# A decoder trunk whose first projection sums the even feature blocks first, and whose last store goes out in two halves

## The chip, the cores and the metric

The kernel runs on one core of one Trainium2 chip. The metric is the time of one execution in device microseconds (us); the time before is the median of 3 runs. PE is the matrix engine, PEld its weight loads, DVE, ACT and POOL are the vector, scalar and general engines, and SP is the engine whose queue issues the kernel's DMAs.

## What is computed

A trunk of two layers over 1024 tokens of width 1024, batch 1. In layer 0 the normalised input is multiplied by one wide matrix, and its columns go to two token mixers; the change touches the first 384 of the columns that feed the attention (queries, keys and values of heads 0 and 1), and the very last addition of layer 1.

```python
def even_mixer(h, w_in, ...):
    z = h @ w_in                       # sum over 1024 features
    u, v, q, k, vb = jnp.split(z, ...)
    ...                                # gMLP of u, v; QK-norm attention of q, k, vb
    return jnp.concatenate([a_out, b_out], axis=-1) @ w_out

def reference(x, ...):
    for layer in range(2):
        h = rms_norm(x, norm_mix_g[layer])
        mix = even_mixer(h, ...) if layer % 2 == 0 else gla_mixer(h, ...)
        x = x + mix
        h = rms_norm(x, norm_ffn_g[layer])
        x = x + conv_ffn(h, ...)
    return x
```

All is float32. A product is made of three passes over parts: each operand is split into a rounded high part and the remainder as a low part, and high by high, high by low and low by high are added up (`PASSES`).

## The kernel before, in words

Tokens are cut into 8 tiles of 128, features into 8 blocks of 128. The program is one long list of instructions that a scheduler orders for each engine before it runs; engines then run their lists strictly in order and wait for one another by semaphores. So a change in one place may re-order the lists for a good way behind it.

**The start.** `x_T` holds each token tile with features on the partitions, even blocks (0, 2, 4, 6) first and odd blocks behind them. `features(n)` (L543 to L552) loads a tile and splits it into `hq[0]` (even blocks) and `hq[1]` (odd blocks), ACT making the high part (L101) and DVE the low part (L102). For the odd halves of tiles 0 and 1 POOL makes the high part. Tile 0 is loaded in two halves (`cut`), tile 1 in one piece. `token_rows(n)` (L536) loads the same tile with tokens on the partitions, and `statistics` squares and sums its rows on ACT (L533), which POOL makes into the scale `r0` of each token (L141, L142). `load_qkv(0, ...)` (L618) loads the first pair's weights in four DMAs of two feature blocks each and scales and splits each block (ACT L106, DVE L107), and calls `between` after each DMA is issued; that hook puts the tile loads between the weight loads. SP issues these DMAs in the order of its list, on one queue.

**The first pair's projection.** `projected(n)` (L773) sums tile n over feature blocks 0 to 7 in `mm_tok` (L193): 8 blocks by 3 passes, 24 matmuls of 128x384 for a tile. Behind it ACT makes the squares and the values (L780, L782), DVE the sums (L787), POOL the scales (L141, L142), DVE and POOL the scaled queries and keys (L789, L791), POOL and DVE their parts `qs` and `ks` (L101, L102). PE turns them (`tq` L809, `tk` L817), makes scores (`sc` L727), turns the exponentials (`pP` L747) and multiplies by the values (`po` L755). `early` lets three tiles be projected ahead of the first unit of attention; `rest` places the row statistics of later tiles. Projections of the next pair fill PE between the units of a pair.

**The end.** `ffn_down` (L384 to L426) makes the last matrix product in seven parts. The last one, part 4 of layer 1, leaves four sums of 128x512, one for each t. Each is added to the residual (DVE, L424) and stored by one DMA on SP (L1272).

## Time and profile before

| what | value |
|---|---|
| runs | 2151.78, 2152.53, 2155.79 us, median 2152.53 |
| the profiled execution, its own time | 2153.15 us |
| its span in the trace | 2151.4 us (1.75 us less) |
| PE busy | 2126.6 us, 99% |
| DVE busy, ACT busy, POOL busy | 1526.0 (71%), 1035.9 (48%), 482.4 us (22%) |
| mean DMA rate | 164 GB/s |
| PE share of the chain that ended last | 92% |

PE is busy all along, apart from the beginning, some short waits and the end. The busy time of the whole span therefore says little about this change: what counts is the first 60 us and the last 4 us. The timeline view gives each group of like instructions on an engine with its start, its length, its count, and in brackets the idle time before it and what ended that. The view of windows gives busy times of stretches, and in the column PEclk the clock that was granted to PE, as a share of full speed.

### The profile page before, as it was taken

To read this page: it belongs to the slowest core of one execution; us is meant where nothing else is said; L and a number is where in the kernel's file an instruction comes from. 1 tells how busy PE (TensorE), PEld (TensorE's weight loads), DVE (VectorE), ACT (ScalarE), POOL (GpSimd) and SP (SyncE) were. 2 spreads that over 40 slices of the span, in tenths; PEclk is the share of its full clock that TensorE was granted. 3 is DMA by queue.
4 is the path that set the end of the run, shared out by engine and by line. 5 is a ranking of instruction groups with operands and counts; after the bars stand their busy time and mean duration, and the time that the engine had idled before them with its cause. 6 is when DMAs were issued, how large, how long until landed. Compare 5 with 4: busy or idle time off the path is not lost.

```text
span 2151.4 us, 29696 instructions
## 1 busy us (share of the span) xinstructions
PE 2126.6 (99%) x10444; PEld 1804.0 (84%) x10444; DVE 1526.0 (71%) x2451; ACT 1035.9 (48%) x1998; POOL 482.4 (22%) x521
## 2 busy tenths in 40 slices
PE   8999999999999999999999999999999999999999
PEld 7999988888888888888898888888788888888887
DVE  7566655587888888655577777677778888885554
ACT  7555664365444444444454455535544444444443
POOL 5344310012424334000010011011234334220000
PEclk9999999999999999999999999999999999999999
DMA  7022313754444544765553233395554544457664
GB/s 273 24 77 68 104 40 120 256 195 156 155 161 158 176 143 157 255 237 192 206 183 113 74 105 102 133 307 206 177 167 161 168 153 154 162 181 280 215 216 166
DMA packets 159413, 353.70 MB, mean 164 GB/s; under 512 B 17392, under 2 KB 54256, under 8 KB 158880
## 3 DMA queue, kind: packets, MB, share of 16 engines
q1 hardware_dynamic: 159264, 351.81, 47.9%
q8 instruction: 82, 1.34, 0.3%
q14 instruction: 67, 0.55, 0.1%
HBM read 243.15 MB, written 108.59 MB: 163 GB/s over the span
## 4 chain that ended last, share of the span: by engine, by line
PE 92%; DVE 2%; ACT 2%; DMA 2%; issue 1%; SPq 0%; POOL 0%; DVEq 0%; ACTq 0%
PE puB L293 11%; PE pgB L293 11%; PE po L193 8%; PE pv L193 6%; PE pj L193 6%; PE puC L293 6%; PE pgC L293 6%; PE pdB L400 5%; PE pdC L400 5%; PE pdO L400 4%; PE puA L293 3%; PE pgA L293 3%; PE pdQ L400 2%; PE pdP L400 2%; PE pu L193 2%; PE pBq L1070 2%
## 5 line engine op out<-in xcount | busy, mean ns | idle before, releaser
L102 DVE TENSOR_TENSOR da<-ar,da 128x512 fp32r<-128x512 f32 x154 | 106.1, 689 | 154.2 <-ACT da L101 154.1
L101 ACT CAST da<-ar 128x512 fp32r<-128x512 f32 x154 | 95.9, 623 | 207.8 <-PE pdC L400 91.5
L193 PE MATMUL po<-wo,hq 128*128 128x512 f32 x768 | 184.0, 394 | 0.2 <-ACT hq L101 0.2
L193 PEld LDWEIGHTS po<-wo,hq 128*128 128x128 f32 x768 | 141.6, 188 | 29.6 <-DVE hq L102 1.1
L193 PE MATMUL pv<-wv,hq 128*128 128x512 f32 (+2 forms) x768 | 140.8, 340 | 1.6 <-DVE b L1102 1.6
L400 PE MATMUL pdB<-dw,da 128*128 128x512 f32 x528 | 135.5, 391 | 0.9 <-ACT u L308 0.7
L400 PE MATMUL pdC<-dw,da 128*128 128x512 f32 x528 | 135.1, 390 | 0.0
L193 PEld LDWEIGHTS pv<-wv,hq 128*128 128x128 f32 x768 | 118.7, 189 | 16.4 <-DVE b L1102 2.1
L400 PEld LDWEIGHTS pdB<-dw,da 128*128 128x128 f32 x528 | 98.7, 188 | 22.3 <-ACT u L308 1.1
L259 POOL TENSOR_TENSOR S1g<-rg 128x512 f32<-128x512 f32 x20 | 31.1, 1555 | 382.9 <-DMA wsd<-D 266.1
L400 PEld LDWEIGHTS pdC<-dw,da 128*128 128x128 f32 x528 | 99.0, 188 | 20.5
L102 DVE TENSOR_TENSOR dw<-wr,dw 128x512 fp32r<-128x512 f32 x154 | 105.6, 686 | 12.1 <-ACT dw L101 11.9
L193 PE MATMUL pj<-wq,hq 128*128 128x384 f32 x576 | 111.3, 341 | 0.0
L141 POOL TENSOR_SCALAR rn<-ssq 128x1 f32<-128x1 f32 x24 | 9.7, 403 | 446.1 <-ACT h L149 244.9
L101 ACT CAST dw<-wr 128x512 fp32r<-128x512 f32 x154 | 95.0, 617 | 15.7 <-DMA wr<-in_w_dn 9.3
L400 PE MATMUL pdO<-dw,da 128*128 128x512 f32 x396 | 102.2, 389 | 0.2 <-DVE dw L102 0.2
L193 PEld LDWEIGHTS pj<-wq,hq 128*128 128x128 f32 x576 | 99.9, 189 | 0.1
L400 PEld LDWEIGHTS pdO<-dw,da 128*128 128x128 f32 x396 | 74.2, 188 | 16.0 <-DVE dw L102 0.6
L322 DVE SCALAR_TENSOR_TENSOR t<-g,cw,t 128x1022 f32<-128x1022 f32 x44 | 76.6, 1742 | 0.1
L306 DVE TENSOR_TENSOR g<-g,s1g 128x512 f32<-128x512 f32 x22 | 16.2, 737 | 76.9 <-ACT s1g L305 76.9
L321 DVE SCALAR_TENSOR_TENSOR t<-g,cw,t 128x1023 f32<-128x1023 f32 x44 | 58.2, 1322 | 16.2 <-ACT t L320 16.1
L323 ACT ACTIVATE t<-t 128x1024 f32<-128x1024 f32 x44 | 46.7, 1061 | 29.7 <-DVE t L322 29.6
(1084 smaller groups left out, 5432.6 us busy)
## 6 DMA issues: line engine op xcount, KB each, us to landing
ar<-actd SPq DMA_DIRECT2D x70, 512.0 KB, 3.5
rd<-in_w_down SPq DMA_DIRECT2D x44, 512.0 KB, 3.6
wsd<-D SPq DMA_DIRECT2D x88, 256.0 KB, 2.3
rg<-in_w_gate SPq DMA_DIRECT2D x42, 512.0 KB, 3.6
ru<-in_w_up SPq DMA_DIRECT2D x42, 512.0 KB, 4.5
wr<-wsd SPq DMA_DIRECT2D x40, 512.0 KB, 4.3
actd<-t SPq DMA_DIRECT2D x66, 256.0 KB, 2.2
wr<-in_w_dn SPq DMA_DIRECT2D x30, 512.0 KB, 4.8
```

Of the source, the lines that this page charges most:

```text
L101: (hi or A.copy)(dst[0], src)
L102: (lo or V.tensor_sub)(dst[1], src, f32(dst[0]))
L141: G.tensor_scalar(r, ssq, 1.0 / n, EPS, op0=ALU.mult, op1=ALU.add)
L193: T.matmul(o, L[i], R[jj][:, sl], start=(k == 0 and (ii, jj) == PASSES[0]), stop=(k == nk - 1 and (ii, jj) == PASSES[-1]))
L259: G.tensor_tensor(sums[name], x, y, op=op)
L293: T.matmul(o, L[ii][:, j * P : j * P + P], right[p][:, jj, j, :], skip_group_check=more, start=(not more and j == 0 and (ii, jj) == PASSES ...
L306: V.tensor_add(C22, C22, s1)
L321: V.scalar_tensor_tensor(t[:, 1:], g[:, : S - 1], w(1), t[:, 1:], op0=ALU.mult, op1=ALU.add)
L322: V.scalar_tensor_tensor(t[:, 2:], g[:, : S - 2], w(0), t[:, 2:], op0=ALU.mult, op1=ALU.add)
L323: A.activation(t, t, AF.Silu)
L400: T.matmul(o, L[ii][:, t * P : t * P + P], R[jj], skip_group_check=more, start=start and not more and (ii, jj) == PASSES[0], stop=stop and ...
L1070: T.matmul(o, L[ii][:, j * P : j * P + P], right[p][:, jj, j, :], skip_group_check=more, start=(not more and j == 0 and (ii, jj) == PASSES ...
```

## The change

The feature blocks of the first pair's weights are stored in the order 0, 2, 4, 6, 1, 3, 5, 7, and the projection of that pair sums in this order. Tile 1, too, is loaded in halves; between the weight loads the halves stand so that the even half of tile 1 comes ahead of both odd halves. The other three pairs keep their order. At the end, the last sum of 128x512 is made as two sums of 128x256, and each is stored by a DMA of its own, the first on SP, the second on ACT's queue, which no DMA of the kernel before uses.

```diff
@@ ffn_down
                 dst = xs[n][:, c * 512 : c * 512 + 512]
+                if l and p == 4 and t == 3:
+                    for i in range(2):
+                        q = slice(i * 256, i * 256 + 256)
+                        V.tensor_add(dst[:, q], dst[:, q], bank[b][t][:, q])
+                        (Q, A)[i].dma_start(rows(out, n)[:, c * 512 + i * 256 : c * 512 + i * 256 + 256], dst[:, q])
+                    continue
                 V.tensor_add(dst, dst, bank[b][t])
@@ even
                 def between(kp):
                     if kp == 0:
                         Q.dma_start(g0, a["norm_mix_gT"])
+                    if kp == 1:
+                        next(tile1)
                         list(tile0)
-                    if kp == 1:
-                        list(features(1))
+                    if kp == 2:
+                        list(tile1)
                     if kp == 3:
                         token_rows(0)
 
                 later = []
-                tile0 = features(0, cut=True)
+                tile0, tile1 = (features(n, cut=True) for n in range(2))
                 next(tile0)
@@ load_qkv
-                src, gain = raw[:, i * 384 : i * 384 + 384], g0[:, k : k + 1]
+                w = (2 * k) % 8 + k // 4 if p == 0 else k
+                src, gain = raw[:, i * 384 : i * 384 + 384], g0[:, w : w + 1]
@@ projected
-                mm_tok([(pj[:, :384], slice(0, 384))], lambda k: tok(n, k),
-                       lambda k: ws[k], KD)
+                mm_tok([(pj[:, :384], slice(0, 384))],
+                       lambda k: tok(n, (2 * k) % 8 + k // 4 if early else k), lambda k: ws[k], KD)
@@ layouts
+    def even_first(m, wanted):
+
+        return np.concatenate([m.reshape(KD, P, -1)[g::2] for g in range(2)]).reshape(m.shape) if wanted else m
...
-        "w_qkv": np.stack([pieces(np.concatenate([cols(m, p, P) for m in (q, k, vb)], 1), 2) for p in range(PAIRS)]),
+        "w_qkv": np.stack([pieces(even_first(np.concatenate([cols(m, p, P) for m in (q, k, vb)], 1), p == 0), 2)
+                           for p in range(PAIRS)]),
```

What this does to the engines' lists is seen at three places. In the rows, a number behind a name tells one buffer from another, and is shifted by one or so between the two kernels, as the line numbers are by up to 14.

The first place is the start. On SP, before, the first loads (`xf` is a token tile by features, 128x512 half of one; `wq00r` to `wq03r` the four weight loads; `g` the gains):

```order
L550 DMA xf_321<-in_x_T 128x512
L111 DMA wq00r<-in_w_qkv 128x768
L556 DMA g_83<-in_norm_mix_gT 128x8
L550 DMA xf_321<-in_x_T 128x512
L111 DMA wq01r<-in_w_qkv 128x768
L547 DMA xf_339<-in_x_T 128x1024
L111 DMA wq02r<-in_w_qkv 128x768
L111 DMA wq03r<-in_w_qkv 128x768
```

And on SP in the changed kernel:

```order
L556 DMA xf_321<-in_x_T 128x512
L111 DMA wq00r<-in_w_qkv 128x768
L562 DMA g_83<-in_norm_mix_gT 128x8
L111 DMA wq01r<-in_w_qkv 128x768
L556 DMA xf_336<-in_x_T 128x512
L556 DMA xf_321<-in_x_T 128x512
L111 DMA wq02r<-in_w_qkv 128x768
L556 DMA xf_336<-in_x_T 128x512
L111 DMA wq03r<-in_w_qkv 128x768
```

The second weight load and the even half of tile 1 now stand ahead of the odd half of tile 0; there is one DMA more, of the same bytes in sum.

On PE at the same place, before, the first matmuls (`hq_85` holds even blocks of tiles 0 to 3, `hq_87` odd ones; `pj_442` is the sum of tile 0, `pj_483` that of tile 1):

```order
L193 MATMUL pj_442<-wx_331,hq_85 128x384 x3
L193 MATMUL pj_442<-wx_334,hq_87 128x384 x3
L193 MATMUL pj_442<-wx_345,hq_85 128x384 x3
L193 MATMUL pj_442<-wx_348,hq_87 128x384
L193 MATMUL pj_483<-wx_331,hq_85 128x384 x2
L193 MATMUL pj_442<-wx_348,hq_87 128x384 x2
```

And on PE in the changed kernel:

```order
L193 MATMUL pj_443<-wx_328,hq_85 128x384 x3
L193 MATMUL pj_443<-wx_331,hq_85 128x384 x3
L193 MATMUL pj_443<-wx_343,hq_85 128x384 x3
L193 MATMUL pj_443<-wx_346,hq_85 128x384
L193 MATMUL pj_484<-wx_328,hq_85 128x384 x2
L193 MATMUL pj_443<-wx_346,hq_85 128x384 x2
L193 MATMUL pj_484<-wx_328,hq_85 128x384
L193 MATMUL pj_484<-wx_331,hq_85 128x384 x3
L193 MATMUL pj_484<-wx_343,hq_85 128x384 x3
L193 MATMUL pj_484<-wx_346,hq_85 128x384 x3
L193 MATMUL pj_443<-wq_0_354,hq_87 128x384 x3
```

Before, the fourth matmul needs odd blocks; now the first 24 need even blocks alone.

The second place is ACT, from the squares of tile 1's rows on (`x_383` and `xk` are tiles with tokens on the partitions; `hq_86`, `hq_88` take tiles 4 to 7; `xf_400` is tile 4, `xf_389` tile 3). Before:

```order
L533 ACTIVATE x_383,ssq_385<-x_383 128x1024
L780 ACTIVATE qn_467<-pj_442,r_84 128x256
L782 ACTIVATE vN_469<-pj_442,r_84 128x128
L533 ACTIVATE xk,ssq_396<-xk 128x1024
L780 ACTIVATE qn_508<-pj_483,r_84 128x256
L782 ACTIVATE vN_510<-pj_483,r_84 128x128
L101 CAST hq_86<-xf_400 128x4x128
L101 CAST hq_88<-xf_400 128x4x128
L101 CAST hq_85<-xf_389 128x4x128
L101 CAST hq_87<-xf_389 128x4x128
```

In the changed kernel, from behind the cast of tile 4 (`xf_408` is tile 5, `xf_390` tile 3):

```order
L101 CAST hq_88<-xf_401 128x4x128
L539 ACTIVATE xk,ssq_472<-xk 128x1024
L101 CAST hq_86<-xf_408 128x4x128
L101 CAST hq_88<-xf_408 128x4x128
L789 ACTIVATE qn_550<-pj_525,r_84 128x256
L791 ACTIVATE vN_552<-pj_525,r_84 128x128
L539 ACTIVATE xk,ssq_513<-xk 128x1024
L101 CAST hq_85<-xf_390 128x4x128
L101 CAST hq_87<-xf_390 128x4x128
```

Up to tile 4 the list is as before; tile 3, whose load moved from the third to the fifth place behind tile 4's on SP, is now cast behind tile 5, the squares and values of tile 2 and two more row statistics.

The third place is PE between the projections of tiles 5 and 6 of the first pair (before `pj_727` and `pj_805`, now `pj_728` and `pj_806`). Before:

```order
L817 MATMUL tk_618<-identr,ks_607 128x128 x4
L193 MATMUL pj_727<-wq_1_370,hq_88 128x384
L727 MATMUL sc0n_627<-kT_440,qT_615 128x128 x2
L727 MATMUL sc0n_634<-kT_440,qT_615 128x128 x2
L809 MATMUL tq_692<-identr,qs_686 128x128 x2
L193 MATMUL pj_805<-wx_331,hq_86 128x384 x3
```

And in the changed kernel, from the scores of tile 0 inside tile 5's projection on:

```order
L736 MATMUL sc0n_635<-kT_441,qT_616 128x128 x2
L818 MATMUL tq_693<-identr,qs_687 128x128 x2
L193 MATMUL pj_728<-wq_0_354,hq_88 128x384
L193 MATMUL pj_728<-wq_1_357,hq_88 128x384 x3
L193 MATMUL pj_728<-wq_0_368,hq_88 128x384 x3
L193 MATMUL pj_728<-wq_1_371,hq_88 128x384 x3
L826 MATMUL tk_699<-identr,ks_688 128x128 x4
L756 MATMUL pP0n_627<-ident,sm0n_631 128x128
L756 MATMUL pP0n_627<-ident,sm0n_638 128x128
L736 MATMUL sc0n_706<-kT_441,qT_696 128x256 x2
L736 MATMUL sc0n_714<-kT_441,qT_696 128x256 x2
L818 MATMUL tq_771<-identr,qs_765 128x128 x2
```

The transposes and scores of tile 0 (`tq`, `tk`, `sc0n`) have moved forward, into the projections of tiles 3 and 5, and the scores of tile 1 stand ahead of tile 6's projection instead of behind tile 7's. Behind this the lists go on in another order through the whole of the attention, up to about 330 us, with the same instructions; after that they are alike but for the last sum and store.

## The prediction

> **What bounds the kernel now.** I read the page first, then PE's waits, then the timeline of the first 60 us and the last 4 us, because the page says that PE is never far from full:

> ```profile
> PE 2126.6 (99%) x10444; PEld 1804.0 (84%) x10444; DVE 1526.0 (71%) x2451; ACT 1035.9 (48%) x1998; POOL 482.4 (22%) x521
> ```

> About 25 us of the span hold no matmul. The view of PE's waits over the first 40 us, and the timeline of PE there (start, length, count), show the largest piece of them:

> ```profile
> PE pj L193 <- ACT wx L106: 5.8, 1, 5.8
> PE pj L193 <- DVE hq L102: 1.4, 1, 1.4
> ...
> 5.79 2.66 PE L193 MATMUL pj<-wx,hq 128*128 128x384 f32 x5 [5.79 <-ACT wx L106]
> 9.86 3.57 PE L193 MATMUL pj<-wx,hq 128*128 128x384 f32 x10 [1.41 <-DVE hq L102]
> ...
> 15.14 1.41 PE L193 MATMUL pj<-wx,hq 128*128 128x384 f32 x7
> 16.39 3.63 PE L193 MATMUL pj<-wq,hq 128*128 128x384 f32 x20
> 19.86 2.24 PE L193 MATMUL pj<-wx,hq 128*128 128x384 f32 x12
> ```

> Only 5 matmuls are made before 9.86. Then two speeds are to be seen. From 16.39 to 19.86 go 20 matmuls, 0.174 us each; from 9.86 to 15.14 go the other 16 (48 for two tiles, less 5, 7 and 20), 0.33 us each. PE starts slow and doubles its speed after 5.3 us of unbroken work. A tile of 24 matmuls is 4.17 us at the fast rate.

> The wait until 9.86 comes from the order of the loads. In the timeline of the other engines:

> ```profile
> 5.12 1.12 ACT L106 ACTIVATE wx<-wq00r,g 128x384 fp32r<-128x384 f32 x2 [0.64 <-DMA g<-in_norm_mix_gT]
> 5.77 1.15 DVE L107 SCALAR_TENSOR_TENSOR wx<-wq00r,g,wx 128x384 fp32r<-128x384 f32 x2 [0.56 <-ACT wx L106]
> 6.57 0.82 POOL L101 CAST hq<-xf 128x512 fp32r<-128x512 f32 x1 [4.39 <-DMA xf<-in_x_T]
> 7.94 1.12 ACT L106 ACTIVATE wx<-wq01r,g 128x384 fp32r<-128x384 f32 x2 [1.69 <-DMA wq01r<-in_w_qkv]
> 8.58 0.62 DVE L107 SCALAR_TENSOR_TENSOR wx<-wq01r,g,wx 128x384 fp32r<-128x384 f32 x1 [1.67 <-ACT wx L106]
> 9.12 0.68 DVE L102 TENSOR_TENSOR hq<-xf,hq 128x512 fp32r<-128x512 f32 x1
> 9.23 1.04 POOL L101 CAST hq<-xf 128x512 fp32r<-128x512 f32 x1 [1.84 <-DMA xf<-in_x_T]
> 10.19 1.12 ACT L106 ACTIVATE wq<-wq02r,g 128x384 fp32r<-128x384 f32 x2 [0.37 <-DMA wq02r<-in_w_qkv]
> ```

> The sixth matmul wants the low part of tile 0's odd blocks. POOL had the high part at 7.39, but DVE stood in its list at the second weight load, which lands at 7.9, and got to it at 9.12.

> **Term A, the start.** The rows give the landings: tile 0's odd half (256 KB) by 6.57, the second weights (384 KB) 7.9, tile 1 (512 KB) 9.2, the third weights (384 KB) 10.2. The changed queue moves the same bytes in another order, so I read each landing off at the same sum of bytes: second weights about 7.0, tile 1's even half 7.9, tile 0's odd half 8.55, third weights 9.5, tile 1's odd half 10.2. ACT needs 0.61 and DVE 0.62 for a block of weights, so blocks 0 to 3 in the new order are split by 8.8, and DVE ends the low part of tile 1's even half at 9.4. PE has matmul 1 at 5.79, 2 at 6.44 and 3 at 6.93, as now (low weights ready at 6.39); the fourth no longer waits. From about 7.25 one matmul follows the other at 0.32 to 0.33. If the fast rate comes after some 5 us as now, near 12, then 17 are done, 7 more even ones last until 13.1; by then the odd halves are there (tile 0's low part comes behind the third weights, 9.5 plus 0.61, 0.62 and 0.68, near 11.4; tile 1's, two weight blocks later, near 13.1), the last low weights by 13.6, and 24 more end at 17.3. Before it was 19.86: **2.6 us earlier**.

> [...]

> **What is given back.** These 2.6 us do not last, since ACT is next. Its timeline, and the window of the same stretch:

> ```profile
> 16.82 1.06 ACT L533 ACTIVATE x<-x 128x1024 f32<-128x1024 f32 x1 [1.98 <-DMA x<-in_x]
> ...
> 18.73 0.47 ACT L780 ACTIVATE qn<-pj,r 128x256 f32<-128x256 f32 x1 [0.77 <-PE pj L193]
> 19.11 0.36 ACT L782 ACTIVATE vN<-pj,r 128x128 f32<-128x128 f32 x1
> 19.36 1.06 ACT L533 ACTIVATE xk<-xk 128x1024 f32<-128x1024 f32 x1
> 20.30 0.20 ACT L533 ACTIVATION_READ_ACCUMULATOR xk<-xk 128x1 f32 x1
> ...
> 21.00 2.19 ACT L101 CAST hq<-xf 128x512 fp32r<-128x512 f32 x4
> ...
> 20.00:24.00 4.00, 4.00 (x25) 4.00 (x24) 3.10 (x6) 4.00 (x9) 3.64 (x6) 1.00 1.03 411
> ```

> The squares of tile 1's rows stand ahead of tile 0's results in ACT's list, and wait for a load that lands at 16.8 in either kernel, as the same bytes are ahead of it. So ACT wins only the 0.77 it waited at 18.73; it then works without pause, and the DMA engines are full too (1.03, 411 GB/s, 1.28 us for 512 KB). Step by step: squares of tile 1 to 18.0, results of tile 0 (0.8) to 18.7, squares (1.25) to 19.9, results of tile 1 to 20.6, cast of tile 4 to 21.7. PE ends tile 2 at 21.5 and finds the first high part of tile 4 at 21.2, the low part (DVE, 0.68) at 21.95: 0.4 us of waiting, tile 4 done near 25.8. Tile 3 is worse off than before, because its load is now the sixth behind 16.8 (six times 1.28, 24.5) and its cast stands behind squares (1.25), tile 5's cast (1.1), tile 2's results (0.8) and squares (1.25): first high part 26.7, low part 27.4. PE waits there for 1.1 us, with 0.3 us of transposes and two matmuls between. Then 22 matmuls and 0.46 us of transposes end at 31.7. Tile 5's projection follows:

> ```profile
> 32.56 2.24 PE L193 MATMUL pj<-wx,hq 128*128 128x384 f32 x12
> ...
> 37.69 0.67 PE L727 MATMUL sc0n<-kT,qT 128*128 128x128 f32 x4 [0.43 <-ACT kT L818]
> ...
> 48.90 0.50 PE L817 MATMUL tk<-identr,ks 128*128 128x128 f32 x4 [0.31 <-ACT qT L812]
> 50.20 0.44 PE L747 MATMUL pP0n<-ident,sm0n 128*128 128x128 f32 x2 [0.80 <-ACT sm0n L733]
> ...
> 52.09 0.50 PE L817 MATMUL tk<-identr,ks 128*128 128x128 f32 x4 [0.31 <-POOL rq L142]
> ...
> 55.85 3.87 PE L193 MATMUL pj<-wq,hq 128*128 128x384 f32 x20
> ```

> It began at 32.56, so **0.9 of the 2.6 us are left** there.

> **Term B, the first units of attention.** Between 32.56 and 55.85, where the second pair's projection starts, PE waits 0.43 + 0.31 + 0.80 + 0.31 = 1.85 us. Worse, it falls back to half its clock:

> ```profile
> 49.30:52.70 3.40, 2.25 (x18) 1.67 (x16) 3.05 (x11) 2.95 (x9) 3.16 (x6) 1.00 0.71 257
> 52.80:56.10 3.30, 3.30 (x19) 3.30 (x18) 2.15 (x6) 1.30 (x7) 0.82 (x3) 0.50 0.16 54
> ```

> The column PEclk (third from the end) is 0.50 right behind the stretch in which PE was busy for 2.25 of 3.40 us; half of 3.3 us, 1.65, is lost. In the new order the transposes and scores of tiles 0 and 1 lie inside or ahead of the projections of tiles 3, 5 and 6, so that no stretch holds small steps alone for so long, and chains through ACT, DVE and POOL have a projection's time to finish. I take the four waits and the slow clock as gone: 3.5 us. One wait is new: the scores of tile 1 follow its transposes at once (37.2), with only the two transposes of exponentials between, while DVE first ends weights and a result and then copies `kT` (to about 38.3): 0.85 us. Bounds: all of the 3.5 stays lost (0), or the new wait does not come either (3.5). **Term B is 2.65 us.**

> [...]

> From 60 to 330 us both lists hold the same work in different order and PE is full in both; I put 0, with 1 us either way. The weights of the next stage that moved on SP's list there have tens of us to spare.

> **Term C, the end.**

> ```profile
> 2147.77 0.69 DVE L424 TENSOR_TENSOR xr<-xr,pdC 128x512 f32<-128x512 f32 x1 [2.71 <-PE pdC L400]
> ...
> 21.24 0.48 DVE L789 SCALAR_TENSOR_TENSOR qn<-pj,r,rq 128x256 f32<-128x256 f32 x1
> ...
> out<-xr SPq DMA_DIRECT2D x16, 256.0 KB, 2.1
> ...
> ogd<-og SPq DMA_DIRECT2D x32, 128.0 KB, 2.2
> ...
> vd<-vN SPq DMA_DIRECT2D x32, 64.0 KB, 1.9
> ```

> A 256-column step that reads sums costs 0.48, so two end 0.1 to 0.25 us after the one of 0.69; the first half is out early, but the second ends the kernel. A store of 256 KB lands after 2.1 us, 128 KB after 2.2, 64 KB after 1.9: half the bytes save 0.3 at most, and may save nothing. ACT's queue shows in no row; by SP's I put it between 0.3 us faster and 0.4 slower. I take **0.1 us gained**.

> **Sum.** 0.9 + 2.65 + 0.1 = 3.65 us. The profiled execution, 2153.15 (span 2151.4 and 1.75 around it), becomes 2149.5. It stood 0.62 above the median, 2152.53, which becomes **2148.9 us**.

> **Rivals.**
> - *The waits only move* (0.22). The new list runs short of ready steps elsewhere, and PE loses as much between tile 5 and the second pair, slow clock included. For: DVE and POOL are nearly full there (third and fifth pair of the window at 49.30: 3.05 and 3.16 of 3.40 us). Against: the new order gives each chain a projection's time. Then 0.9 + 0.1 remain: 2151.5.
> - *More goes* (0.20). The new wait is hidden and the longer lead lets later waits of the attention vanish too, about 1 us: 3.65 + 0.85 + 1, 2147.0.
> - *Slower* (0.10): the half clock comes at new places. Around 25.8 to 27.4 PE now waits 1.1 us between small steps, and again near 37 to 40; each such fall costs 1.65. If the old one stays, Term B is 0 and one fall gives 2151.5 + 1.65 = 2153.2, two 2154.8, three 2156.5. The point from which it decides is the second fall.
> - *It does not do what it says*: if the second weights land at 7.9 after all (order of queue without effect), PE stops after 6 matmuls until 8.6, and A shrinks by 1 us; since ACT hides that at 18.0, the sum is as forecast. It needs no case of its own.

> **Chances and range.** Forecast 0.48 (2147.8 to 2150.5), the others as given. 0.2% is 4.3 us, about what a measurement of this kernel can tell from no change. Faster by more than that (under 2148.2) are the second rival and a third of the forecast: 0.36; slower (over 2156.8) only three falls and more: 0.04; within it 0.60. The range takes in the first two rivals with 1 us for the attention behind 60, and one fall: 2146.2 to 2153.0.

> **What would show it.** In the changed profile: matmuls unbroken from about 7.3, tile 2 beginning near 17.3; ACT without its wait of 0.77; a wait of PE ahead of tiles 4 and 3 for casts; tile 5 at about 31.7; the second pair's projection near 52.3; PEclk of 1.00 throughout 45 to 60; the last DMA's landing as late after the last matmul as now. I am wrong if the head start of 2.6 us is still there at tile 5, or if 0.50 stands in PEclk again.

## The result and the profile after

The changed kernel takes 2149.76 us, median of 21 runs (2147.00 to 2152.46), where the kernel before took 2152.92 on the same chip (21 runs, 2151.25 to 2157.86). The medians lie 3.2 us apart, 0.15%. The ratio estimated from all the runs is 0.9982, with a 95% interval from 0.9975 to 0.9988, which is 2.6 to 5.4 us less. The forecast was 2148.9, the range 2146.2 to 2153.0. The profiled execution took 2149.27 us, with a span of 2147.4, 4.0 less than the profiled one of before.

The page's first rows, as before in the order engine, busy time, share:

```profile
span 2147.4 us, 29707 instructions
...
PE 2125.2 (99%) x10444; PEld 1803.5 (84%) x10444; DVE 1530.4 (71%) x2452; ACT 1034.8 (48%) x1998; POOL 482.3 (22%) x521
```

PE makes the same 10444 matmuls. It is idle for 22.2 us where it was for 24.8, and busy for 1.4 us less, in part because 17 matmuls instead of 22 start ahead of its full clock, where one takes about 0.32 us instead of 0.174.

PE's timeline of the first 54 us (start, length, count, and in brackets the wait before):

```profile
5.66 7.30 PE L193 MATMUL pj<-wx,hq 128*128 128x384 f32 x24 [5.66 <-ACT wx L106]
12.79 4.33 PE L193 MATMUL pj<-wq,hq 128*128 128x384 f32 x24
16.96 2.24 PE L193 MATMUL pj<-wx,hq 128*128 128x384 f32 x12
...
21.12 2.36 PE L193 MATMUL pj<-wx,hq 128*128 128x384 f32 x12
...
25.54 2.68 PE L193 MATMUL pj<-wx,hq 128*128 128x384 f32 x12
...
30.52 2.25 PE L193 MATMUL pj<-wx,hq 128*128 128x384 f32 x12
...
37.34 0.73 PE L736 MATMUL sc0n<-kT,qT 128*128 128x256 f32 x4 [1.00 <-DVE kT L827]
...
39.12 3.76 PE L193 MATMUL pj<-wx,hq 128*128 128x384 f32 x12
...
46.57 2.35 PE L193 MATMUL pj<-wx,hq 128*128 128x384 f32 x12 [0.52 <-DVE qn L798]
...
53.98 3.88 PE L193 MATMUL pj<-wq,hq 128*128 128x384 f32 x21
```

The 48 matmuls of tiles 0 and 1 show no wait between them (first two rows), and tile 2 begins at 16.96 instead of 19.86. Twelve matmuls at the fast clock take 2.24 us. The groups of tiles 4 and 3 (21.12 and 25.54) take 2.36 and 2.68: by this difference PE waits for 0.12 and 0.44 us inside these groups, which no bracket shows. Tile 5 begins at 30.52 (32.56 before), the second pair's projection at 53.98 (55.85). The group at 39.12 is the one to look at: 3.76 us for work of 2.25. The windows around it, with PEclk third from the end:

```profile
35.43:38.84 3.41, 2.35 (x19) 1.84 (x18) 3.41 (x10) 2.79 (x10) 3.21 (x6) 1.00 0.81 225
38.84:42.25 3.41, 3.41 (x14) 3.41 (x14) 2.08 (x6) 2.32 (x7) 3.23 (x7) 0.50 0.42 131
```

So the half clock of before, at 52.74, is not gone. It now comes at 38.84, right behind the new wait of 1.00 us for `kT`, and again lasts 3.41 us; the stretch from 49.3 to 56.1, where it was, now has 1.00.

At the end, the timeline:

```profile
2140.20 3.56 PE L400 MATMUL pdC<-dw,da 128*128 128x512 f32 x15
...
2143.80 0.75 DVE L427 TENSOR_TENSOR xr<-xr,pdC 128x256 f32<-128x256 f32 x2 [2.71 <-PE pdC L400]
2144.25 0.33 SPq L428 DMA_DIRECT2D out<-xr  x1
2144.58 0.37 ACTq L428 DMA_DIRECT2D out<-xr  x1
```

And the DMAs of the last 10 us (queue, count, size, us from issue to landing):

```profile
out<-xr SPq DMA_DIRECT2D x1, 256.0 KB, 2.0
out<-xr SPq DMA_DIRECT2D x1, 128.0 KB, 1.9
out<-xr ACTq DMA_DIRECT2D x1, 128.0 KB, 1.8
```

The two half sums take 0.75 us where the whole one took 0.69. Half a store lands after 1.9 us on SP and after 1.8 on ACT's queue, a whole one after 2.0. From the end of the last matmul to the end of the span it is 3.67 us; before it was 3.66.

Read off at the same places in all profiled executions (us from the span's start; tile 2, tile 5 and the second pair begin with the 49th, 121st and 193rd matmul of the projections `pj`; the first gate matmul is the first that writes `pgB` in layer 0, long behind everything that the change moves; the experiments are told below):

| kernel | full clock from | tile 2 | tile 5 | half clock | second pair | first gate matmul | from there to the last matmul |
|---|---|---|---|---|---|---|---|
| before | 15.20 | 19.86 | 32.56 | 52.74 | 55.85 | 469.3 | 1678.4 |
| changed | 11.54 | 16.96 | 30.52 | 38.84 | 53.98 | 465.6 | 1678.2 |
| changed, a second time | 11.46 | 17.11 | 30.45 | 38.77 | 53.89 | 466.0 | 1681.1 |
| start alone | 10.13 | 16.49 | 30.39 | none | 52.34 | 464.4 | 1679.5 |
| end alone | 12.73 | 18.73 | 31.43 | 50.28, twice as long | 55.60 | 469.7 | 1679.8 |
| new loads alone | 16.75 | 21.37 | 34.36 | 54.29 | 57.30 | 472.8 | 1679.3 |
| new sums, old loads | 11.13 | 17.15 | 30.15 | none | 52.88 | 466.0 | 1678.9 |
| kT on ACT | 12.84 | 18.05 | 31.13 | none | 52.37 | 464.0 | 1677.5 |
| 8 transposes ahead | 11.18 | 16.84 | 30.77 | none | 52.73 | 464.6 | 1679.2 |
| 16 transposes ahead | 8.99 | 16.36 | 30.34 | none | 52.29 | 464.2 | 1682.1 |
| 8 ahead and kT on ACT | 11.21 | 16.90 | 30.51 | none | 52.06 | 464.7 | 1680.7 |
| 32 transposes ahead | 7.88 | 15.95 | 31.83 | 250.23 and 376.52 | 50.91 | 477.8 | 1680.2 |
| 32 ahead, rows first | 5.97 | 15.92 | 30.62 | 40.10 | 52.39 | 467.0 | 1682.0 |

The last column is work that no edit here touches, yet it scatters by 4.6 us from one execution to the next. That is as much as the whole effect, so single times and even medians of 11 runs say little of one microsecond at the start; the columns ahead of it say more. They scatter too: the end alone has the same lists as the kernel before up to its last sum, and begins tile 2 at 18.73 where that began it at 19.86.

### The profile page after: what moved, and what is told of

It is laid out like the page before. It is cut to its first block, busy times and chain, and to the rows that moved or that the text cites. A ratio compares the mean times of both kernels' runs of the same rounds, so it can differ in the third digit from the quotient of the medians.

```text
span 2147.4 us, 29707 instructions
## 1 busy us (share of the span) xinstructions
PE 2125.2 (99%) x10444; PEld 1803.5 (84%) x10444; DVE 1530.4 (71%) x2452; ACT 1034.8 (48%) x1998; POOL 482.3 (22%) x521
## 4 chain that ended last, share of the span: by engine, by line
PE 89%; DMA 4%; DVE 3%; ACT 3%; issue 1%; POOL 0%; SPq 0%; DVEq 0%; ACTq 0%
PE puB L293 11%; PE pgB L293 11%; PE pv L193 6%; PE pgC L293 6%; PE puC L293 6%; PE pj L193 5%; PE pdB L400 5%; PE pdC L400 5%; PE po L193 5%; PE pdO L400 4%; PE puA L293 3%; PE pgA L293 3%; PE pdQ L400 2%; PE pdP L400 2%; PE pu L193 2%; PE pBq L1079 2%
## 5 line engine op out<-in xcount | busy, mean ns | idle before, releaser
L102 DVE TENSOR_TENSOR da<-ar,da 128x512 fp32r<-128x512 f32 x154 | 106.3, 690 | 155.9 <-ACT da L101 155.7
L101 ACT CAST da<-ar 128x512 fp32r<-128x512 f32 x154 | 95.9, 623 | 210.4 <-PE pdC L400 91.6
L193 PE MATMUL po<-wo,hq 128*128 128x512 f32 x768 | 184.0, 394 | 0.2 <-ACT hq L101 0.2
L193 PEld LDWEIGHTS po<-wo,hq 128*128 128x128 f32 x768 | 141.7, 188 | 29.5 <-DVE hq L102 1.1
L193 PE MATMUL pv<-wv,hq 128*128 128x512 f32 (+2 forms) x768 | 140.9, 340 | 1.6 <-DVE b L1111 1.6
L400 PE MATMUL pdB<-dw,da 128*128 128x512 f32 x528 | 135.5, 391 | 1.0 <-ACT u L308 0.7
L400 PE MATMUL pdC<-dw,da 128*128 128x512 f32 x528 | 135.1, 390 | 0.0
L193 PEld LDWEIGHTS pv<-wv,hq 128*128 128x128 f32 x768 | 118.8, 189 | 16.3 <-DVE b L1111 2.1
L193 PE MATMUL pj<-wq,hq 128*128 128x384 f32 x576 | 120.3, 345 | 0.1
L400 PEld LDWEIGHTS pdB<-dw,da 128*128 128x128 f32 x528 | 98.7, 188 | 22.4 <-ACT u L308 1.1
L400 PEld LDWEIGHTS pdC<-dw,da 128*128 128x128 f32 x528 | 99.1, 188 | 20.5
L102 DVE TENSOR_TENSOR dw<-wr,dw 128x512 fp32r<-128x512 f32 x154 | 105.8, 687 | 10.3 <-ACT dw L101 10.2
L400 PE MATMUL pdO<-dw,da 128*128 128x512 f32 x396 | 102.2, 389 | 0.2 <-DVE dw L102 0.2
L101 ACT CAST dw<-wr 128x512 fp32r<-128x512 f32 x154 | 95.0, 617 | 13.6 <-DMA wr<-in_w_dn 7.6
L193 PEld LDWEIGHTS pj<-wq,hq 128*128 128x128 f32 x576 | 97.5, 188 | 0.5 <-DVE qn L798 0.4
L400 PEld LDWEIGHTS pdO<-dw,da 128*128 128x128 f32 x396 | 74.3, 188 | 15.9 <-DVE dw L102 0.6
## 6 DMA issues: line engine op xcount, KB each, us to landing
wsd<-D SPq DMA_DIRECT2D x88, 256.0 KB, 2.3
actd<-t SPq DMA_DIRECT2D x66, 256.0 KB, 2.2
```

The costliest lines, as they stand in the source:

```text
L101: (hi or A.copy)(dst[0], src)
L102: (lo or V.tensor_sub)(dst[1], src, f32(dst[0]))
L193: T.matmul(o, L[i], R[jj][:, sl], start=(k == 0 and (ii, jj) == PASSES[0]), stop=(k == nk - 1 and (ii, jj) == PASSES[-1]))
L400: T.matmul(o, L[ii][:, t * P : t * P + P], R[jj], skip_group_check=more, start=start and not more and (ii, jj) == PASSES[0], stop=stop and ...
```

## The experiments

### Which part brings it: the start alone, the end alone

The first kernel is the changed one without the halves of the last sum and store, the second is the kernel before with them.

```diff
-                if l and p == 4 and t == 3:
-                    for i in range(2):
...
-                    continue
                 V.tensor_add(dst, dst, bank[b][t])
```

> The changed kernel without the halves at its end; the start is as changed. Theory: the whole gain comes from the order of sums and loads in the first 60 us, the halves bring 0.1 us; so about 2149.9 us, 3.1 us under the kernel before. Rival: the two halves on two queues bring 1 us or more at the end; then 2150.8 us or above, and the time from the last matmul to the end of the span is over 0.5 us longer than in the changed kernel (3.63 us there).

> The kernel before with only the last sum and store in halves. Theory: no difference that can be measured, 2152.8 us, and from the last matmul to the end of the span 3.6 us as in both kernels. Rival (the halves bring 1 us or more): 2151.9 us or below.

The start alone took 2149.91 us (11 runs), ratio 0.9986 (0.9977 to 0.9995); the end alone 2154.70, ratio 1.0004 (0.9995 to 1.0012). From the last matmul to the span's end it was 3.60 and 3.51 us. What the change brings comes from the start; the halves bring nothing that shows. (The kernel before ran beside each group of experiments, with medians from 2152.75 to 2153.97 us, so the ratios compare the kernels better than the times.)

The start alone has the changed kernel's lists up to the end, and the same wait for `kT`. But it has no half clock. PE's timeline of that stretch, and then its windows, cut where the clock's steps lie:

```profile
37.21 0.74 PE L730 MATMUL sc0n<-kT,qT 128*128 128x256 f32 x4 [1.00 <-DVE kT L821]
...
38.91 2.32 PE L193 MATMUL pj<-wx,hq 128*128 128x384 f32 x12
...
52.34 1.98 PE L193 MATMUL pj<-wq,hq 128*128 128x384 f32 x10
```

```profile
34.03:37.43 3.40, 2.34 (x15) 1.93 (x14) 3.40 (x12) 2.51 (x8) 2.92 (x5) 1.00 0.93 278
37.43:40.85 3.42, 3.42 (x25) 3.28 (x25) 2.93 (x9) 2.79 (x9) 3.19 (x9) 1.00 0.68 197
```

Tile 6's twelve matmuls take 2.32 us instead of 3.76, and the second pair begins at 52.34, 1.6 us ahead of the changed kernel's. Up to the last sum the two kernels have the same lists, so they differ there in nothing but the microsecond at which things happen.

### The two halves of the start

The first of these sums in the new order and has the new order of weights, but loads as before. The second loads in the new order, while weights and sums stay as before.

```diff
                 def between(kp):
...
-                    if kp == 1:
-                        next(tile1)
                         list(tile0)
-                    if kp == 2:
-                        list(tile1)
+                    if kp == 1:
+                        list(features(1))
...
```

> The sum and the weights in the new order, the loads in the old one (tile 0's odd half ahead of the second weights, tile 1 in one piece). Theory: PE now runs from its first matmul without a break, so each part of a us by which it starts later is lost: the second weights land at 7.9 instead of 7.0, tile 1's even half at 9.2 instead of 7.9, PE stands for some 1 to 1.5 us between 7.3 and 10, and the kernel takes 2150.5 to 2151.3 us. Rival (the prediction's view: ACT's list, held up by the load of tile 1's rows at 16.7, sets the pace behind the start): PE makes up for it by tile 4, and the time is that of the changed kernel, 2149.8 within 0.4 us.

> The loads in the new order, weights and sums in the old one. Theory (the order of the sums makes the gain, the order of loads none by itself): the fourth to sixth matmuls of a tile want odd blocks, which now land later and are split by DVE behind the third weights, near 11.4; PE runs without a break from there instead of from 9.86, and the kernel takes 2153.5 to 2154.5 us, slower than before. Rival (the loads make the gain): 2150 to 2151.5 us.

New sums with old loads: 2151.01 us, ratio 0.9991 (0.9982 to 0.9999). The time lies where it was expected, but not for the reason given. PE did not stop for the later loads:

```profile
6.07 0.69 PE L193 MATMUL pj<-wx,hq 128*128 128x384 f32 x1 [6.07 <-ACT wx L106]
6.96 6.18 PE L193 MATMUL pj<-wx,hq 128*128 128x384 f32 x23 [0.20 <-DVE wx L107]
12.99 4.32 PE L193 MATMUL pj<-wq,hq 128*128 128x384 f32 x24
17.15 2.24 PE L193 MATMUL pj<-wx,hq 128*128 128x384 f32 x12
```

The old order costs the start next to nothing: 17.15 against 16.96, and 17.11 in the second execution of the changed kernel. At 0.32 us for a matmul, PE comes to the seventh, the first that needs the second weights, at 8.41. The loads also came sooner than expected: the second weights were in use from 7.24 and tile 1's even half from 8.64, where 7.9 and 9.2 had been assumed. Whether the kernel is slower than the changed one at all is open, as the intervals overlap. What its trace loses, it loses later: its lists behind the start came out differently, with waits of 1.30 us at 35.7, 0.90 at 48.1 and 0.31 at 50.1. Its second pair begins 0.54 us behind that of the start alone, which has no half clock either, and with 0.81 us of products (`po`) not yet done that stand ahead there.

New loads with old sums: 2155.51 us, ratio 1.0014 (1.0005 to 1.0023), slower than before, as expected and by somewhat more. PE's timeline shows why:

```profile
5.87 1.66 PE L193 MATMUL pj<-wx,hq 128*128 128x384 f32 x3 [5.87 <-ACT wx L106]
8.56 2.25 PE L193 MATMUL pj<-wx,hq 128*128 128x384 f32 x5 [1.03 <-ACT hq L101]
12.26 2.61 PE L193 MATMUL pj<-wx,hq 128*128 128x384 f32 x7 [1.46 <-DVE hq L102]
```

The fourth matmul still wants odd blocks, which now arrive later; two stops of 1.03 and 1.46 us, the full clock 1.55 us later, tile 2 at 21.37. So it is the order of the sums, with that of the weights which goes with it, that carries the gain at the start. The order of the loads alone costs, and together with the new sums it moves little.

### When the half clock falls

First the changed kernel again, for a single profiled execution; then 8 float32 transposes, or 16 of the rounded kind, put ahead of PE's list into a bank that is free by then. Their result is not used, and all other lists stay as they are in the changed kernel, row for row. They are meant to shift the microsecond at which the clock rises, and nothing else.

```diff
+                warm = ps.tile([P, 4, P], F32, tag="pt", name="warm")
+                for i in range(8):
+                    T.transpose(warm[:, i % 4, :], ident, ident)
```

> The changed kernel once more, for a second look at its clock. Theory: the lists, the waits of 1.0 and 0.5 us at 36 and 45 us come again as they were, but whether PE falls to half its clock between them differs from one execution to the next with the phase of whatever counts its idle time; the second pair's projection starts at 52.3 without the fall and near 54.0 with it. Rival: the fall belongs to this list, and is there at 38 to 43 us again.

> The changed kernel with 8 float32 transposes of the identity ahead of PE's list, into a bank that is free at that time; their result is not used. All other lists are as in the changed kernel, row for row. Theory (PE's slow first microseconds set when tile 2 begins, and the clock looks back over some 3.4 us of PE's work): 8 transposes are about 2 us of work and end 1.5 us or more before the first matmul, so they bring at most a part: fast rate from 10 to 11.5 us (now 11.54), tile 2 from 16.3 to 17.0 (now 16.96). Of what is won ACT's and the loads' order gives a part back: tile 5 at 30.0 to 30.5. Time 2149.0 to 2149.8. Rival (any work ahead of the first matmul restarts the clock's climb at once): fast from 8 to 9, tile 2 near 16.0, tile 5 at 29.7, time 2148.5 to 2149.

> The same with 16 transposes of the rounded float32 kind, which take about 0.11 us each when PE is slow: about 2 us of work as well, ending at another time. Theory: as the one before, fast from 10 to 11.5, tile 2 from 16.3 to 17.0, time 2149.0 to 2149.8. Rival: fast from 8 to 9, tile 2 near 16.0, time 2148.5 to 2149. In both runs the half clock shows in PEclk where the stretch of transposes and scores at 35 to 39 us falls into one step of the clock, and does not where a step parts it; with it the second pair starts 1.6 us later.

Again: 2152.70 us for the one execution, with the waits of 1.00 and 0.54 us and the half clock from 38.77 to 42.18. Eight transposes: 2150.88 us, ratio 0.9984 (0.9975 to 0.9994). Sixteen: 2152.64, ratio 0.9997 (0.9988 to 1.0006). Neither median lies in the expected range (2149.0 to 2149.8). The interval of 16 takes in 1: by its times this kernel is not told from the kernel before, though in its trace the second pair begins 3.6 us earlier. It started earlier than the kernel with 8 and has the higher median, but their intervals overlap; its profiled execution reached the first gate matmul at 464.2, 1.4 us ahead of the changed kernel's, and lost 3.9 us in the part behind it that is the same in both. On the full clock the theory was right for 8 transposes (11.18); with 16 it came where the rival had it (8.99), while tile 2 began at 16.36, where the theory had it. But the step of 3.41 us that ended at 8.99 began at 5.58, just ahead of the first product at 5.68, so it holds products all along; where the step lies is enough to explain it (in the changed kernel the full clock followed such a step too, 8.13 to 11.54), and that the 16 transposes raised the clock is not shown. They took 2.27 us, 0.14 each, where 0.11 had been expected.

For the half clock these runs are the clearest. With 8 transposes, PE's timeline, and the windows cut at the clock's steps:

```profile
1.69 1.97 PE L574 MATMUL warm<-ident 128*128 128x128 f32 x8 [1.69 <-POOL ident masks.py:199]
...
30.77 2.24 PE L193 MATMUL pj<-wx,hq 128*128 128x384 f32 x12
...
37.56 0.74 PE L739 MATMUL sc0n<-kT,qT 128*128 128x256 f32 x4 [1.02 <-DVE kT L830]
...
39.27 2.32 PE L193 MATMUL pj<-wx,hq 128*128 128x384 f32 x12
...
52.73 3.88 PE L193 MATMUL pj<-wq,hq 128*128 128x384 f32 x21
```

```profile
35.07:38.48 3.41, 2.34 (x18) 1.92 (x18) 3.41 (x11) 2.57 (x9) 3.27 (x5) 1.00 0.86 220
38.48:41.89 3.41, 3.41 (x23) 3.27 (x23) 2.53 (x8) 2.92 (x8) 3.19 (x9) 1.00 0.57 186
```

The wait is there (1.02), the second wait too (0.53), tile 5 is even 0.25 us later than in the changed kernel, and still the second pair begins 1.25 us earlier, because tile 6's matmuls ran at the full clock. From tile 5 to the second pair it is 23.46 and 23.44 us in the two executions of the changed kernel, and 21.95, 21.96 and 21.95 with the start alone, with 8 and with 16 transposes: the fall costs 1.5 us. In every trace here that has a fall, the rise and the fall lie a whole number of steps of 3.41 us apart (11.54 to 38.84 is eight of them, 15.20 to 52.74 eleven). Whether a fall comes goes with where the steps cut the program: five executions with these lists have the wait of 1.0 us, and two of them, whose step covers 35.4 to 38.8, fell; but five executions are few. What in a step decides it is not shown; that it is PE's idle time, or its work over some 3.4 us, was assumed in the expectations above. PE's busy time does not part the cases: 2.34 us did not fall here, 2.35 and 2.39 did. The time of the weight loads does for this stretch (1.84 and 1.87 us fell, 1.92 and 1.93 did not), but a step of the changed kernel that begins at 1165.24 has 1.78 and 1.14 us of the two, with a wait of 1.63, and no half clock follows it (its trace shows none between 42.25 and the last matmul).

### Taking the wait for `kT` away

In the first pair, ACT instead of DVE copies `kT` of tile 1; then the same with the 8 transposes ahead. The scheduler also moves some steps of the lists here: on PE, four products (`po0n`) now stand ahead of the scores of tile 1.

```diff
-                (V.tensor_copy if n % 2 else A.copy)(four(kT), by4(f32(tk)))
+                (V.tensor_copy if n % 2 and (p or n > 1) else A.copy)(four(kT), by4(f32(tk)))
```

> The changed kernel with one copy moved: the keys of tile 1 of the first pair are copied from PSUM by ACT instead of DVE, whose list holds two weight blocks and a result ahead of that copy. Theory: the wait of 1.0 us ahead of tile 1's scores (36.3 to 37.3 us) comes from this copy, and the half clock from 38.8 to 42.3 us from this wait; both go, 2.7 us in a profile that had both, so 2147.1 to 2148.3 us and PEclk of 1.00 from 30 to 60 us. Rival: the units of attention are short of ready work whatever copies the keys, and the wait comes back at the next step (the copy of the exponentials or the next transposes); then 2149.2 to 2149.8 us, with the half clock still there.

> Both at once: the 8 transposes ahead and the copy of the first pair's kT of tile 1 on ACT instead of DVE; apart from the transposes all lists are as in the run with that copy on ACT alone. If the parts add, tile 2 begins at 16.3 to 17.0, the waits between tile 5 and the second pair sum to about 0.9 instead of 1.5, no 0.50 stands in PEclk, the second pair starts by 52.0 and its first gate matmul by 464; time 2148.0 to 2149.5. If only the rest of the program decides (its time scatters by 4 us between executions), the median is 2149.5 to 2150.5 and not to be told from the changed kernel's.

The copy on ACT: 2150.03 us, ratio 0.9985 (0.9976 to 0.9994), not told apart from the changed kernel's and above what was expected. Both: 2151.20, ratio 0.9995 (0.9986 to 1.0004), above both expected ranges, and not told from the kernel before by its times. In the traces the wait went as it should. Of the first:

```profile
31.13 2.24 PE L193 MATMUL pj<-wx,hq 128*128 128x384 f32 x12
...
37.31 0.66 PE L764 MATMUL po0n<-vN,pT0n 128*128 128x64 f32 x4 [0.68 <-DVE pT0n L761]
37.78 0.72 PE L736 MATMUL sc0n<-kT,qT 128*128 128x256 f32 x4
...
38.83 2.35 PE L193 MATMUL pj<-wx,hq 128*128 128x384 f32 x12 [0.21 <-DVE qn L798]
...
52.37 0.94 PE L193 MATMUL pj<-wq,hq 128*128 128x384 f32 x4
```

The waits sum to 0.89 us instead of 1.52. No half clock shows, but three executions with the wait have none either, so that the wait causes the fall is not shown; from tile 5 to the second pair it is 21.24 us, in the kernel with the start alone 21.95, in the changed one 23.46. Both edits together bring the second pair to 52.06, the earliest but for the kernel with 32 transposes below. But the gate matmul comes at 464.0 and 464.7, with the start alone at 464.4, and the time does not fall. So none of these versions is shown to be faster than the change itself.

### PE's slow start taken away

With 32 rounded transposes PE works from 2.1 to 6.4 us; that this brings the full clock by the time the first product comes was the author's assumption. A second kernel, planned together with the first, also loads the rows of tile 1 ahead of the two small loads of gains, so that ACT's squares start earlier. In both, the lists behind the start come out in another order.

```diff
+                warm = ps.tile([P, 4, P], F32R, tag="pt", name="warm")
+                for i in range(32):
+                    T.transpose(warm[:, i % 4, :], identr, identr)
...
+                    token_rows(n - 1)
...
-                    token_rows(n - 1)
```

> The changed kernel with 32 transposes of the identity of 128x128 put ahead of the first matmul, into a bank that nothing reads, so that PE has worked for 3.5 us when the first operands are there. Theory: the slow rate of PE (0.32 us for a matmul until 11.5) hides the loads in the changed kernel. With the fast rate from the start PE stands for loads and splits: even blocks done by 10.8, the odd ones held by DVE's last weight blocks (13.9), tile 2 begins at 15.7 instead of 16.5 to 17.0, and at tile 4 PE waits 0.7 us or more for ACT's cast (20.6, its list held by the load of tile 1's rows), so 0.5 us at most are left there: 2149.2 to 2149.8 us. Rival: PE is the bound from the first matmul on and all that the slow rate costs there (17 matmuls by 0.15, 2.5 us) is gained: 2147.3 us.

> As the run before, and the rows of tile 1 are loaded ahead of the two small broadcast loads of the query and key gains, which take about 1.1 us of the queue. Theory (ACT's list, held by the load of tile 1's rows, is next behind loads): the squares of tile 1 begin near 15.6 instead of 16.7, tile 4's cast ends 1 us earlier, the wait of PE ahead of tile 4 is gone, and another 0.5 to 1 us is gained: 2148.3 to 2149.0 us. Rival (the list of the first units of attention is the bound, and takes back what comes early): no difference to the run before.

The first took 2165.16 us, ratio 1.0056 (1.0043 to 1.0068), the second 2152.95, ratio 1.0002 (0.9993 to 1.0010); neither is what theory or rival gave. The start itself came near what was expected: tile 2 at 15.95 and 15.92 for 15.7. The full clock came at 7.88 in the first, 1.7 us behind the first product, and at 5.97 in the second, ahead of it. The loss of the first lies far from the start, in PE's waits between 60 and 470 us:

```profile
PE sc3n L739 <- DVE ot3n L744: 4.0, 1, 4.0
PE pc L718 <- DMA cat<-bcat: 2.6, 1, 2.6
PE pc L451 <- DMA cat<-bcat: 1.5, 1, 1.5
```

The scheduler had ordered the whole attention anew, and its end (the scores `sc3n`, and the products `pc` on columns that come back by DMA) is late by 8 us of new waits, with two falls to the half clock behind them. This says nothing against a warm start; it shows what a reshuffled list can cost. The second kernel does not lose there, but has waits of 0.46 us (twice) and 1.28 us ahead of its own transposes and scores, and a half clock at 40.10. Of the earlier start, tile 2 a whole us ahead of the changed kernel, little was left at tile 5: 30.62 against 30.52, with 0.39 us of scores done ahead of it.

## Why the prediction was right, and where it was not

The total was right: 3.65 us forecast, 3.88 between the two profiled executions, 3.2 between the medians. But three of its steps were wrong and nearly cancel: 1.1 us too much was given back behind the start, 1.0 us came behind 60 us where nothing had been put, and Term B was 2.3 us too high. So the sum owes part of its accuracy to luck. So does the agreement of the two profiled executions: the second one of the changed kernel, which took 2152.70, needed 2.9 us more behind the first gate matmul.

**Term A, the start: right.** 2.6 us were forecast, 2.90 came. Of the landings read off at equal bytes, four were good to 0.3 us, as the first use of each shows (tile 1's even half 7.9 forecast, 7.67 measured; tile 0's odd half 8.55 and 8.46; the third weights 9.5 and 9.42; tile 1's odd half 10.2 and 10.12). The second weights were 0.9 us earlier: 7.0 forecast, in use from 6.12. That changed nothing, since PE comes to the matmul that needs them only at 8.07. The matmuls run every 0.32 us until 11.3, as forecast, and the full clock came at 11.54 instead of near 12. But the run with old loads shows that the careful order of loads, on which much of that working was spent, hardly mattered to the start: with matmuls at 0.32 us PE never came to stand for it.

The size of the term hangs on one execution of the kernel before. The end alone has the same lists up to its last sum, and PE's stop there ends at 9.83, as before at 9.86; but its clock rose at 12.73 instead of 15.20, and from its timeline:

```profile
18.73 2.24 PE L193 MATMUL pj<-wx,hq 128*128 128x384 f32 x12
...
31.43 2.24 PE L193 MATMUL pj<-wx,hq 128*128 128x384 f32 x12
```

The three executions with the changed start have 16.49 to 17.11 at tile 2 and 30.39 to 30.52 at tile 5. So the start brings from 1.6 to 3.4 us, according to which two executions are compared, and 0.9 to 2.2 us of it are left at tile 5.

**What is given back: the first step that failed.** "0.9 of the 2.6 us are left" at tile 5; between the two profiled executions 2.04 were left, and 0.29 us of transposes (`tk`) had been done besides. Against the end alone 0.9 were left, so this difference alone would not settle it; but tile 5 itself, forecast for 31.7, began at 30.39 to 30.52 in all three executions, 1.2 us earlier. Both waits came where they were forecast, but with 0.12 and 0.44 us instead of 0.4 and 1.1. I had added up the durations of ACT's rows; the timeline of ACT in the changed kernel shows that they overlap:

```profile
16.67 1.06 ACT L539 ACTIVATE x<-x 128x1024 f32<-128x1024 f32 x1 [1.94 <-DMA x<-in_x]
17.63 0.18 ACT L539 ACTIVATION_READ_ACCUMULATOR x<-x 128x1 f32 x1
17.72 0.46 ACT L789 ACTIVATE qn<-pj,r 128x256 f32<-128x256 f32 x1
18.08 0.36 ACT L791 ACTIVATE vN<-pj,r 128x128 f32<-128x128 f32 x1
18.33 1.05 ACT L539 ACTIVATE xk<-xk 128x1024 f32<-128x1024 f32 x1
...
19.98 1.15 ACT L101 CAST hq<-xf 128x512 fp32r<-128x512 f32 x2
...
24.75 1.15 ACT L101 CAST hq<-xf 128x512 fp32r<-128x512 f32 x2
```

From one start to the next, squares with their read take 1.05 us (17.72 less 16.67), not 1.25, and a tile's results 0.61 (18.33 less 17.72), not 0.8. So the cast of tile 4 begins at 19.98 where 20.6 was forecast, and that of tile 3, five such steps later, at 24.75; its first half, 0.62 us, is done by 25.4, which I had at 26.7. No wait for its load shows, which I had landing at 24.5. Mechanism and place were right, and the size was off. The rows of the kernel before had shown it already: there a tile's results take 0.63 us from start to start (18.73 to 19.36).

**Term B, the first units of attention: the other step that failed.** "I take the four waits and the slow clock as gone", 2.65 us net. The second pair begins 1.87 us earlier, and 0.81 us of products (`po`) that stood behind its start now stand ahead: 2.68 in all, of which 2.33 were there at tile 5. Term B brought 0.35 between these two executions. The four waits did go and the one for `kT` came as forecast (1.00 for 0.85), but a second one came that I had not seen, 0.52 for the scaled queries (`qn`) ahead of tile 7, and the half clock fell again, 14 us earlier. Of the two signs that I had named against myself, 0.50 in PEclk has come; the other, the head start still there at tile 5, came in great part between these two executions (2.04 of 2.90). Where it does not fall (the start alone), the term is 55.85 less 52.34 and 0.81 of products, 4.32, less 2.46 there at tile 5: 1.86 us. The argument that no stretch holds small steps alone for so long was wrong at 35 to 39 us, and the rival that named 37 to 40 us as a new place for the fall had seen it. It was priced at 1.65; the runs show 1.5.

**From 60 us on.** 0 within 1 was forecast; the first gate matmul is 3.68 us earlier, 1.0 more than what stood at the second pair: the edge of that range. The waits of 0.82 and 0.26 us late in the attention are gone, others of 0.32, 0.19 and 0.12 have come, which accounts for less than half of it; where the rest comes from was not found. Behind the gate matmul 0.3 us are left to the scatter.

**Term C, the end.** 0.1 forecast, nothing measured: from the last matmul to the span's end it is 3.67 and 3.51 us with the halves (changed, end alone), 3.66 and 3.60 without (before, start alone). By the rows, the second half's sum and issue take back what its smaller store saves (1.8 instead of 2.0 us).

**The rivals.** "The waits only move" describes what happened between tile 5 and the second pair, but not the time, since more was left of the start. "Slower" needed a second fall, and only one came. In two of the experiments, a small edit did make the kernel slower (new loads alone, and 32 transposes), by mechanisms that were in none of the rivals.

## What to carry to other kernels

A wait at the start of a list is worth what is left of it at the next place where another engine or a load sets the pace: follow that engine's list row by row, with distances from start to start and not with sums of durations. Before a load is moved, look whether the consumer is slow enough to hide its old place. And judge such a change by marks along the trace, where a microsecond can be seen, since the medians of a 2 ms program with 4 us of scatter can hardly show a single one. Take these marks from more than one execution of each kernel: here two kernels with the same lists, whose clocks rose at 15.20 and 12.73, began tile 2 at 19.86 and 18.73, 1.1 us apart.

## What the runs showed of the hardware

```profile
6.80:11.30 4.50, 4.50 (x16) 4.50 (x16) 3.04 (x5) 2.43 (x5) 1.63 (x2) 1.00 1.00 369
```

  In it go about 14 matmuls, one every 0.32 us; behind 11.58 one goes every 0.174. So at the start of these two traces the distance of the matmuls shows the slow rate, and the column does not.
- **What sets the 4.6 us of scatter behind the first gate matmul** is not shown; one of its pieces is in the second execution of the changed kernel, a fall to the half clock at 1523.57 us (PEclk 0.50 for 3.41 us), where the first execution and the kernel before have 1.00 from 1523.5 to 1526.9.
